# Differences of later sets made in the attentions and the second half's rings, and the mix's gating one product later

## The chip, the cores and the metric

The kernel runs on one core of one Trainium2 chip, all in float32. The metric is the device time of one execution in microseconds (us): 1691.08, the median of three runs (1689.67 to 1693.02).

## The reference

One layer of a decoder trunk: sequence 2048, width 1024, 16 query heads and 2 key/value heads of 64, window 128. A modulation of x by the condition c comes first, then one wide projection, an attention and a pooling branch side by side, a gated mix of the two, an output projection and a LayerNorm.

```python
shift, scale, gate = split(silu(c) @ w_ada + b_ada, 3)
u = x * (1 + scale) + shift
q, k, v, a_gate, p_in, p_gate, m_a, m_p = split(u @ w_in, offsets)
a = sliding_window_sink_attention(q, k, v, sinks, bias, mask) * silu(a_gate)
a = a @ w_attn_proj
p = grouped_linear(multiscale_causal_pool(p_in), w_pool_mix)
p = (p * pool_scale * silu(p_gate)) @ w_pool_proj
y = sigmoid(m_a) * a + sigmoid(m_p) * p
y = (y @ w_out) * (1 + gate)
x = layer_norm(alpha * x + y, ln_gain, ln_bias)
```

## The kernel before

**Products.** Every float32 operand is split into a high and a low part, and a product is three matmuls for each of four blocks of 128 rows, 12 of 128x512 in all (`product`, L317). The high part is a cast on ScalarE; the low part, source minus high part, is a subtraction on VectorE or GpSimd (`low`, L131; `pair_split`, L304; `half_split`, L310).

**Seven products for eight.** Matrices are multiplied two by two in blocks, with sums and differences of blocks, so that seven products do for eight. The activations are the "sets" B11, T1, T2, B21, T3, B22 and T4, each of which holds a high and a low part; T1 to T4 are differences of the blocks B11, B12, B21 and B22. The weights' differences are made on GpSimd (`sum1` L269, `mid` L273 and L274, `late` L278). The results stand in banks of PSUM, four called mm and two called lg. Some additions on VectorE stand between the products: `b = c + p5` after T2 (L368) and `p5 = c + p5` after T3 (L390). T3 and T4 add into the bank c that these additions read, so the next product into c waits for them.

**Sets from memory.** The inputs of later stages lie in device memory as blocks: `ain_d` (attention times its gate), `pin_d` (pool), `wo_d` (the output projection's weights), each in four slices. `sums_to` (L199) makes the differences of one slice: it loads four blocks of 256 KB into two tiles called spare, makes T1, T2, T4 and T3 as four subtractions of 128x512 on GpSimd, and stores each. `set_steps` (L509) loads and splits a finished set shortly before its stage.

**Stages.** The sequence is worked in two halves, s = 0 and 1:

1. Head, and the first half's rings: gates, keys, values and the first queries.
2. Attention of half 0 (`attention`, L774). It runs 67 steps n; one step is a block of scores, softmax, transposes and values for one pair of heads. Between these, 13 "fills" (products for pool, queries and merge gates) are spread evenly, 93 products in all. Each fill's weights are split up to three products ahead (`splits`).
3. The second half's rings (`second_phase`, L1465), five groups of 14 ticks; a tick is the end of one product. Beside the products, side work hangs on given ticks (`hooks`): here `sums_to` for all slices of `ain_d[0]` and `pin_d[0]`, and the scaling of `wo` by 1 + gate.
4. Attention of half 1.
5. The mix (from L1560): six phases. The first finishes the gates; then the attention's and the pool's projections for half 0 and for half 1 (two groups of 14 ticks each); then the output projection and the norm. Its side work before is `sums_to` for `ain_d[1]`, `pin_d[1]` and `wo_d`, one slice every 8 ticks from tick 2.

**Order.** The compiler's scheduler orders an engine's instructions by its own estimate. Operations called through `pe`, `act`, `dve`, `pool` and `sp` (class `Ordered`, L51) are pinned behind the instruction that was written before them for that engine; those called as `nc.vector` or `nc.scalar` are free. All loads and stores named here are issued by the queue of SP, in order. An engine works its instructions in order, and one that waits holds those behind it. `defer(k, f)` writes f k ticks later; `later(n, f)` in the attention writes f at step n.

**Gating in the mix.** In `attn_quad` (L611) a product's result is multiplied by its sigmoid gate into a tile `wide` (L618); in `pool_quad` (L622) it is multiplied by its gate (L627) and added to `wide` (L629), which is then stored. Both are called at the tick at which the product ends. The gates are loaded by `gates_ahead` (L599), which writes the sigmoid (L607) right after the load. In `back` (L341) two such quads make a group, in the order T2, B21 for each, then T3, B22 for each, then T4 for each.

Of the kernel before, what the change touches and what calls it, by code (L numbers as in the profile page):

```python
# [60 lines left out]
def kernel(  # L61
# [137 lines left out]
    def sums_to(ph, store, i, load, work=None, sums=True):  # L199

        b = []

        def x(r, c):
            return b[r][:, c * CH : (c + 1) * CH]

        def fetch():
            b.extend((ph.spare(), ph.spare()))
            b.reverse()
            for r in (1, 0):
                load(b[r], r)  # L210

        def sub(out, a, c):
            return lambda: pool.tensor_tensor(x(*out), x(*a), x(*c), ALU.subtract)

        todo = [(0, fetch)]
        if work:
            todo += [(3, lambda: work(b[0], 0)), (3.5, lambda: work(b[1], 1))]
        made = [("B11", (0, 0)), ("B21", (1, 0)), ("B22", (1, 1))] if work else []
        if work and not sums:
            made.insert(1, ("B12", (0, 1)))  # L220
        puts = [(5 + 0.6 * n, *x) for n, x in enumerate(made)]
        if sums:
            at = 7.5 if work else 4
            for out, a, c, name in (
                ((0, 1), (0, 1), (0, 0), "T1"),
                ((1, 1), (1, 1), (0, 1), "T2"),
                ((1, 0), (1, 0), (1, 1), "T4"),
                ((0, 0), (1, 1), (0, 0), "T3"),
            ):
                todo.append((at, sub(out, a, c)))  # L230
                puts.append((at + 2.5, name, out))
                at += 1.5
# [108 lines left out]
    def back(ph, grp, opened, nxt, own, tick):  # L341
# [5 lines left out]
        for q, (a, b, c, w, *copy) in zip(grp, opened):  # L347
# [19 lines left out]
            if len(copy) < 2:  # L367
                nc.vector.tensor_tensor(b, c, p5, ALU.add)  # L368
# [17 lines left out]
        def with_t3(x):  # L386
# [3 lines left out]
            nc.vector.tensor_tensor(p5, c, p5, ALU.add)  # L390
# [14 lines left out]
        for q, b, c, p5 in st:  # L405
            w = half_split(ph, q.a22)
            product(c, w, "T4")
            tick()
            q.consume(ph, 1, 0, c)

# [188 lines left out]
    def gates_ahead(name, s, m, raw):  # L599
        g = {}  # L600

        def ahead(ph, turn):
            for mi, t in (((0, 0), (1, 1)), ((0, 1), (1, 0)))[turn]:
                x = g[mi, t] = ph.c("g")
                sp.dma_start(x, gates_d[name][s, m + mi, t])
                if raw:
                    nc.scalar.activation(x, x, AF.Sigmoid)  # L607

        return g, ahead

    def attn_quad(s, m):  # L611
        g, ahead = gates_ahead("ma", s, m, True)

        def consume(ph, mi, t, src):
# [3 lines left out]
            nc.vector.tensor_tensor(ta[k][:, t * CH : (t + 1) * CH], src, g.pop((mi, t)), ALU.mult)  # L618

        return Quad((wap[m], wap[m + 1]), consume, ahead)  # L620

    def pool_quad(s, m):  # L622
        gates, ahead = gates_ahead("mp", s, m, True)

        def consume(ph, mi, t, src):
            g = gates.pop((mi, t))
            nc.vector.tensor_tensor(g, src, g, ALU.mult)  # L627
            dst = ta[m + mi][:, t * CH : (t + 1) * CH]
            nc.vector.tensor_tensor(dst, g, dst, ALU.add)  # L629
            defer(3, lambda: sp.dma_start(y_d[s, m + mi, t], dst))  # L630

        return Quad((wpp[m], wpp[m + 1]), consume, ahead)
# [141 lines left out]
    def attention(ph, s, fills, post, opened):  # L774
# [690 lines left out]
    def second_phase(ph, opened, post, plan1):  # L1465
# [37 lines left out]
        hooks.setdefault((3, 0), []).append(lambda: ph.turns.clear())  # L1503
# [57 lines left out]
    with Pools("mix", spare=4, p=2, c=8) as ph:  # L1561
# [92 lines left out]
```

## Time and profile before

| what | us |
|---|---|
| median of three runs | 1691.08 |
| the profiled execution | 1693.3 |
| its span, first to last instruction | 1691.5 |
| TensorE busy | 1648.7 |
| VectorE busy | 1193.7 |
| ScalarE busy | 1030.0 |
| GpSimd busy | 988.5 |

In the rows of the profile PE is TensorE's matmul, PEld its load of weights, DVE VectorE, ACT ScalarE, POOL GpSimd, SP the engine that issues DMAs (SPq its queue). A row of a timeline gives the start in us from the span's start, the length, engine, line, operation, the tile written and those read, shapes, and how many such instructions are merged; in brackets the idle time of the engine before it and what ended that. A row of the busy times by stage gives the stage, its length, the busy time of PE, PEld, DVE, ACT and POOL (with counts), the granted share of TensorE's clock, the share of the DMA engines and GB/s. Line 57 stands for everything called through `Ordered`. The first attention runs from about 254 to 600 us, the second half's rings to 824, the second attention to 1176, the mix to the end.

### The profile page before, as it was taken

The page shows a single profiled execution, that of the slowest core. Times are in us where ns is not written, and L with a number is a line of the kernel's source. Part 1 is how long each engine was busy: PE and PEld are TensorE (multiplying, and loading weights), DVE is VectorE, ACT ScalarE, POOL GpSimd, SP SyncE. Part 2 cuts the span into 40 slices and gives each one's busy share as a digit, 9 for nine tenths or more (in the row PEclk, how much of TensorE's full clock was granted, in tenths as well). Part 3 has the DMA queues.
Part 4 walks back from the last instruction along what each step waited for, and adds up shares of the span by engine and source line. Part 5 has one row for each costly group of instructions (what it writes and reads, how often), then busy time and mean ns, then how long its engine had stood idle before and what let it go on. Part 6 is the DMA issues. An engine that isn't in the chain of part 4 may idle for free.

```text
span 1691.5 us, 24675 instructions
## 1 busy us (share of the span) xinstructions
PE 1648.7 (97%) x8058; PEld 1384.4 (82%) x8058; DVE 1193.7 (71%) x2132; ACT 1030.0 (61%) x2150; POOL 988.5 (58%) x734
## 2 busy tenths in 40 slices
PE   7999999999999999999999999999999999999997
PEld 6788888888888888888788888888878777887886
DVE  6856545676857657357567677676669897989877
ACT  4755457878778755335578777876646445644452
POOL 3343437586857828762476867496567576533442
PEclk9999999999999999999999999999999999999999
DMA  9688843343432478766533344234979797888443
GB/s 359 219 279 307 197 161 102 101 132 108 149 107 99 135 248 308 267 231 211 190 114 99 114 130 156 81 114 135 336 247 363 262 360 259 318 283 271 150 150 112
DMA packets 188849, 336.79 MB, mean 199 GB/s; under 512 B 18336, under 2 KB 44080, under 8 KB 188720
## 3 DMA queue, kind: packets, MB, share of 16 engines
q1 hardware_dynamic: 185600, 330.96, 57.3%
q10 hardware_dynamic: 3088, 4.23, 1.0%
q8 instruction: 64, 1.05, 0.2%
q14 instruction: 65, 0.53, 0.1%
q0 software_dynamic: 32, 0.02, 0.0%
HBM read 227.96 MB, written 110.33 MB: 200 GB/s over the span
## 4 chain that ended last, share of the span: by engine, by line
PE 74%; DVE 8%; DMA 7%; ACT 4%; issue 3%; POOL 3%; SPq 1%; POOLq 0%; DVEq 0%; ACTq 0%
PE mm L57 48%; PE lg L57 19%; PE pv L57 4%; PE pt L57 4%; DVE w_set L132 1%; DMA ain_T<-spare 1%; ACT L L57 1%; DMA g<-ma_d 1%; DMA g<-mp_d 1%; DVE w_set L57 1%; DVE set_T L57 1%; POOL W L269 1%; DMA spare<-pin_B 1%; DVE L L57 1%; ACT w_set L57 1%
## 5 line engine op out<-in xcount | busy, mean ns | idle before, releaser
L57 PE MATMUL mm<-set_B,w_set 128*128 128x512 f32 x2664 | 655.8, 393 | 2.2 <-DVE w_set L132 1.2
L57 PEld LDWEIGHTS mm<-set_B,w_set 128*128 128x128 f32 x2664 | 497.1, 189 | 107.0 <-DVE w_set L132 2.4
L57 PE MATMUL mm<-set_T,w_set 128*128 128x512 f32 x1824 | 455.5, 396 | 5.9 <-DVE mm L57 3.9
L57 PE MATMUL lg<-set_T,w_set 128*128 128x512 f32 x1704 | 412.6, 392 | 10.5 <-DVE p L390 4.4
L57 PEld LDWEIGHTS mm<-set_T,w_set 128*128 128x128 f32 x1824 | 336.7, 189 | 76.2 <-DVE mm L57 6.5
L57 PEld LDWEIGHTS lg<-set_T,w_set 128*128 128x128 f32 x1704 | 319.9, 189 | 81.8 <-ACT w_set L306 5.2
L132 DVE TENSOR_TENSOR w_set<-W,w_set 128x1024 fp32r<-128x1024 f32 x137 | 197.8, 1445 | 142.3 <-ACT w_set L306 129.3
L306 ACT CAST w_set<-W 128x1024 fp32r<-128x1024 f32 x137 | 143.8, 1050 | 212.7 <-PE mm L57 124.3
L57 POOL TENSOR_TENSOR w_set<-W,w_set 128x512 fp32r<-128x512 f32 x120 | 157.3, 1318 | 116.9 <-ACT w_set L57 112.0
L269 POOL TENSOR_TENSOR W<-W,A 128x512 f32<-128x512 f32 x46 | 74.1, 1610 | 232.5 <-DMA A<-in_win_dram 63.5
L57 DVE TENSOR_TENSOR o<-pv,o 64x128 f32<-64x128 f32 x256 | 72.1, 282 | 133.7 <-ACT o L57 127.3
L57 POOL TENSOR_TENSOR spare<-spare 128x512 f32<-128x512 f32 x68 | 124.0, 1826 | 31.5 <-DMA spare<-pin_B 12.2
L57 POOL TENSOR_TENSOR W<-W 128x512 f32<-128x512 f32 x82 | 108.3, 1336 | 53.2 <-DVE sm L57 31.0
L57 ACT ACTIVATE L<-L,nm 128x257 f32<-128x257 f32 (+1 forms) x256 | 127.2, 499 | 9.3 <-DVE nm L57 3.7
L278 POOL TENSOR_TENSOR W<-W 128x512 f32<-128x512 f32 x46 | 72.8, 1583 | 95.9 <-DVE w_set L132 83.5
L57 DVE CUSTOM_DVE_ANT_0 L<-lg,bt,nsink 128x256 f32<-128x256 f32 (+1 forms) x256 | 111.7, 473 | 21.3 <-PE lg L57 11.9
L57 ACT CAST w_set<-W 128x512 fp32r<-128x512 f32 (+1 forms) x165 | 101.4, 628 | 20.9 <-POOL W L57 14.9
L273 POOL TENSOR_TENSOR W<-W 128x512 f32<-128x512 f32 x44 | 72.7, 1656 | 66.3 <-DVE w_set L132 57.2
L57 ACT COPY o<-pv 64x256 f32<-64x256 f32 x128 | 47.4, 370 | 75.9 <-PE pv L57 74.7
L57 DVE TENSOR_TENSOR ptl<-pt,pth 128x512 fp32r<-128x512 f32 (+1 forms) x128 | 85.7, 669 | 1.3 <-ACT pth L57 1.0
L274 POOL TENSOR_TENSOR W<-W 128x512 f32<-128x512 f32 x44 | 71.6, 1628 | 21.9 <-DMA W<-in_win_dram 18.9
L57 ACT ACTIVATE L<-L,sm 128x256 f32<-128x256 f32 (+1 forms) x128 | 64.3, 502 | 31.7 <-DVE sm L57 31.4
(230 smaller groups left out, 2398.2 us busy)
## 6 DMA issues: line engine op xcount, KB each, us to landing
W<-in_win_dram SPq DMA_DIRECT2D x42, 512.0 KB, 5.4
W<-in_win_dram SPq DMA_DIRECT2D x42, 256.0 KB, 3.7
A<-in_win_dram SPq DMA_DIRECT2D x42, 256.0 KB, 4.9
ag_d<-sig SPq DMA_DIRECT2D x32, 256.0 KB, 5.7
pg_d<-sig SPq DMA_DIRECT2D x32, 256.0 KB, 4.4
pg<-pg_d SPq DMA_DIRECT2D x32, 256.0 KB, 3.2
pin_B<-fin SPq DMA_DIRECT2D x32, 256.0 KB, 2.0
ag<-ag_d SPq DMA_DIRECT2D x32, 256.0 KB, 2.9
```

Of the source, the lines that this page charges most:

```text
L57: return lambda *args, **kw: self.tc.keep_in_program_order(op(*args, **kw))
L132: engine.tensor_tensor(dst, src, as32(hi), ALU.subtract)
L269: e.tensor_tensor(self.w[:, 1, :], self.w[:, 2, :], self.a22, ALU.add)
L273: e.tensor_tensor(x[:, 1, :], x[:, 1, :], x[:, 0, :], ALU.subtract)
L274: e.tensor_tensor(x[:, 2, :], x[:, 0, :], x[:, 2, :], ALU.subtract)
L278: e.tensor_tensor(x[:, 3, :], x[:, 3, :], x[:, 1, :], ALU.subtract)
L306: a.copy(by_two(hi), raw)
```

## The change

Four things change:

- **Where differences are made.** In each attention, `sums_to` now runs for three of the four slices of that half's `ain_d`, from steps 39, 56 and 61, at half a step for a tick. Its two tiles are the places of two query tiles (qs00, qs01). The second half's rings make the fourth slice of `ain_d[0]`, all of `pin_d[0]`, and now the differences of `wo` too, with other start ticks. The mix keeps only the fourth slice of `ain_d[1]` and the four of `pin_d[1]`, one every 14 ticks from tick 11. The tiles borrowed in the rings are given back a group earlier.
- **Start of an attention.** The first two splits are written ahead of the copy `seed(0)` and the load of the Exp table, the third behind the copy p5.
- **Gating in the mix.** A product's gating is written when the next product is consumed (`one_behind`), the last one at the first tick after the group. Gatings, and the additions L368 and L390 in these groups, are pinned.
- **Small steps.** The sigmoid is written a tick later than the load of its gate; y is stored two ticks after the gating rather than three.

```diff
-    def sums_to(ph, store, i, load, work=None, sums=True):
+    def sums_to(ph, store, i, load, work=None):
...
-            todo += [(3, lambda: work(b[0], 0)), (3.5, lambda: work(b[1], 1))]
+            todo += [(4, lambda: work(b[0], 0)), (4.5, lambda: work(b[1], 1))]
...
     def back(ph, grp, opened, nxt, own, tick):
...
-                nc.vector.tensor_tensor(b, c, p5, ALU.add)
+                (dve if q.ahead else nc.vector).tensor_tensor(b, c, p5, ALU.add)
...
-            nc.vector.tensor_tensor(p5, c, p5, ALU.add)
+            (dve if q.ahead else nc.vector).tensor_tensor(p5, c, p5, ALU.add)
...
             q.consume(ph, 1, 0, c)
+        defer(1, use_up)
...
-                    nc.scalar.activation(x, x, AF.Sigmoid)
+                    defer(1, lambda x=x: nc.scalar.activation(x, x, AF.Sigmoid))
...
+    unused = []
+
+    def use_up():
+        while unused:
+            unused.pop()()
+
+    def one_behind(use):
+
+        def consume(ph, mi, t, src):
+            use_up()
+            unused.append(lambda: use(ph, mi, t, src))
+
+        return consume
...
-            nc.vector.tensor_tensor(ta[k][:, t * CH : (t + 1) * CH], src, g.pop((mi, t)), ALU.mult)
+            dve.tensor_tensor(ta[k][:, t * CH : (t + 1) * CH], src, g.pop((mi, t)), ALU.mult)
-        return Quad((wap[m], wap[m + 1]), consume, ahead)
+        return Quad((wap[m], wap[m + 1]), one_behind(consume), ahead)
...
-            nc.vector.tensor_tensor(g, src, g, ALU.mult)
+            dve.tensor_tensor(g, src, g, ALU.mult)
             dst = ta[m + mi][:, t * CH : (t + 1) * CH]
-            nc.vector.tensor_tensor(dst, g, dst, ALU.add)
-            defer(3, lambda: sp.dma_start(y_d[s, m + mi, t], dst))
+            dve.tensor_tensor(dst, g, dst, ALU.add)
+            defer(2, lambda: sp.dma_start(y_d[s, m + mi, t], dst))
-        return Quad((wpp[m], wpp[m + 1]), consume, ahead)
+        return Quad((wpp[m], wpp[m + 1]), one_behind(consume), ahead)
...
         bts = {0: bias_tile(0)}
+        for i in (-3, -2):
+            for j in splits.get(i, ()):
+                split(j)
+        seed(0)
         act.activation(warm, mhalf, AF.Exp)
-        seed(0)
         p5 = st[0][3] = tp.tile([P, CH], F32, tag="p5", bufs=2, name="p5")
         act.copy(p5, st[0][1])
-        for i in range(-3, 0):
-            for j in splits.get(i, ()):
-                split(j)
+        for j in splits.get(-1, ()):
+            split(j)
+
+        def sums_between(n0, i):
+            for offset, f in [(0, rooms), *sums_to(ph, ain_d[s], i, load_raw(ain_d[s], i))]:
+                later(n0 + int(offset / 2), f)
+
+        def rooms():
+            ph.turns["spare"] = iter([kvp.tile([P, D], F32, tag=f"qs0{t}", name=f"room{t}") for t in range(2)])
+
+        for i, n0 in enumerate((39, 56, 61)):
+            sums_between(n0, i)
...
-        for raw in (ain_d[0], pin_d[0]):
-            for i in range(4):
-                side.append(sums_to(ph, raw, i, load_raw(raw, i)))
+        for raw, i in ((ain_d[0], 3), *((pin_d[0], i) for i in range(4))):
+            side.append(sums_to(ph, raw, i, load_raw(raw, i)))
...
-                False,
...
-        for start, todo in zip((14, 18.5, 23, 27.5, 32, 36.5, 41, 45.5, 57, 61, 65, 69), side):
+        for start, todo in zip((14, 18, 22, 26, 30, 34, 39, 44, 50), side):
...
-        hooks.setdefault((3, 0), []).append(lambda: ph.turns.clear())
+        hooks.setdefault((2, 0), []).append(lambda: ph.turns.clear())
...
-        for n, (raw, i) in enumerate((raw, i) for raw in (ain_d[1], pin_d[1], wo_d) for i in range(4)):
+        for n, (raw, i) in enumerate([(ain_d[1], 3), *((pin_d[1], i) for i in range(4))]):
             for offset, f in sums_to(ph, raw, i, load_raw(raw, i)):
-                at = int(2 + 8 * n + offset)
+                at = int(11 + 14 * n + offset)
```

More of the change, by code (lines that the diff above doesn't have):

```diff
@@ L216, in sums_to @@
         if work:
-            todo += [(3, lambda: work(b[0], 0)), (3.5, lambda: work(b[1], 1))]
+            todo += [(4, lambda: work(b[0], 0)), (4.5, lambda: work(b[1], 1))]
         made = [("B11", (0, 0)), ("B21", (1, 0)), ("B22", (1, 1))] if work else []
-        if work and not sums:
-            made.insert(1, ("B12", (0, 1)))
         puts = [(5 + 0.6 * n, *x) for n, x in enumerate(made)]
[L222 to L232, printed above, removed]
+        at = 7.5 if work else 4
+        for out, a, c, name in (
+            ((0, 1), (0, 1), (0, 0), "T1"),
+            ((1, 1), (1, 1), (0, 1), "T2"),
+            ((1, 0), (1, 0), (1, 1), "T4"),
+            ((0, 0), (1, 1), (0, 0), "T3"),
+        ):
+            todo.append((at, sub(out, a, c)))
+            puts.append((at + 2.5, name, out))
+            at += 1.5
         for at, name, z in puts:
```

## The prediction

> **What bounds the kernel now.** I read the page first, then the list of TensorE's waits, then the busy time by stage, then the timeline around each place where TensorE stood. The page:
>
> ```profile
> span 1691.5 us, 24675 instructions
> PE 1648.7 (97%) x8058; PEld 1384.4 (82%) x8058; DVE 1193.7 (71%) x2132; ACT 1030.0 (61%) x2150; POOL 988.5 (58%) x734
> ```
>
> TensorE is the bound. The change takes no product away, so all it can give or cost is time in which TensorE stands, or runs at less than the full clock. The waits of PE alone (us in total, times, longest), and then the stages in which PE is not full (length; PE busy; DVE, ACT, POOL; granted clock; DMA):
>
> ```profile
> PE lg L57 <- DVE p L390: 4.4, 3, 2.2
> PE lg L57 <- DVE w_set L132: 4.0, 1, 4.0
> PE mm L57 <- DVE mm L57: 3.9, 4, 1.6
> ```
>
> ```profile
> 254.00:265.00 11.00, 9.58 (x39) 7.44 (x38) 1.46 (x7) 6.39 (x15) 7.38 (x6) 0.84 0.27 75
> 265.00:560.00 295.00, 291.95 (x1591) 251.49 (x1590) 207.53 (x589) 228.73 (x637) 211.74 (x175) 1.00 0.36 115
> 560.00:600.00 40.00, 39.18 (x211) 33.26 (x211) 25.80 (x69) 26.95 (x70) 31.21 (x25) 1.00 0.43 141
> 600.00:824.00 224.00, 224.00 (x995) 185.34 (x994) 136.00 (x131) 103.75 (x148) 119.23 (x78) 1.00 0.75 256
> 824.00:835.00 11.00, 9.71 (x44) 7.45 (x43) 2.86 (x8) 7.24 (x14) 6.07 (x6) 1.00 0.49 162
> 835.00:1135.00 300.00, 297.72 (x1632) 256.89 (x1631) 213.15 (x591) 234.42 (x643) 213.82 (x170) 1.00 0.36 115
> 1135.00:1176.00 41.00, 40.56 (x220) 34.77 (x220) 27.07 (x69) 27.07 (x70) 31.27 (x25) 1.00 0.41 135
> 1215.00:1250.00 35.00, 30.77 (x124) 24.50 (x123) 28.26 (x24) 18.93 (x25) 22.24 (x13) 0.90 0.85 302
> 1320.00:1335.00 15.00, 12.76 (x50) 10.12 (x49) 14.86 (x16) 2.10 (x2) 11.57 (x8) 0.89 0.85 287
> 1370.00:1416.00 46.00, 43.48 (x187) 34.38 (x187) 42.42 (x36) 21.39 (x29) 30.18 (x17) 1.00 0.79 281
> 1520.00:1530.00 10.00, 8.52 (x38) 6.78 (x37) 9.93 (x12) 3.15 (x3) 2.91 (x2) 1.00 1.05 361
> ```
>
> What a stage loses is its length less PE's busy time, plus the share of the clock that was not granted. In the mix that gives 4.23 + 0.10 x 35 = 7.7 us, 2.24 + 0.11 x 15 = 3.9, 2.5 and 1.5: together 15.6. The start of the first attention (254 to 265) loses 1.42 + 0.16 x 11 = 3.2, that of the second (824 to 835) 1.3. The rest of the attentions loses 3.05 + 0.82 + 2.28 + 0.44 = 6.6, and the second half's rings (600 to 824) nothing. So the change has about 20 us to win, and most of it lies in the mix.
>
> The clock's part can be doubted. The Trainium skill (TensorE: Matmul & The Clock Gate, Part 1) has the clock halved only after an idle window of about 3.4 us; by it a stall of 2.24 us, the one in 1320 to 1335, would cost no clock, and the sum below would be 1.7 us smaller. The row with 0.89 says that this one did, and I go by the row.
>
> **What the mix waits for.** Timeline of the largest stall (start, us, engine):
>
> ```profile
> 1209.01 1.23 DVE L132 TENSOR_TENSOR w_set<-W,w_set 128x1024 fp32r<-128x1024 f32 x1 [2.27 <-ACT w_set L306]
> ...
> 1227.50 4.52 POOL L57 TENSOR_TENSOR spare<-spare 128x512 f32<-128x512 f32 x2
> ...
> 1228.56 2.31 DVE L132 TENSOR_TENSOR w_set<-W,w_set 128x1024 fp32r<-128x1024 f32 x1
> ...
> 1235.90 1.27 DVE L618 TENSOR_TENSOR wide<-mm,g 128x512 f32<-128x512 f32 x2
> ...
> 1237.10 0.67 DVE L390 TENSOR_TENSOR p<-lg,p 128x512 f32<-128x512 f32 x1
> 1237.81 0.69 DVE L618 TENSOR_TENSOR wide<-p,g 128x512 f32<-128x512 f32 x1
> ...
> 1238.41 2.28 DVE L132 TENSOR_TENSOR w_set<-W,w_set 128x1024 fp32r<-128x1024 f32 x1
> ...
> 1240.75 2.07 PE L57 MATMUL lg<-set_T,w_set 128*128 128x512 f32 x4 [4.00 <-DVE w_set L132]
> ```
>
> Two things make VectorE late here. Three gatings (1.27 + 0.69 us) and an addition stand in its queue before the low part (1238.41) for which TensorE waits. And that low part takes 2.28 us, as does the one at 1228.56 beside a GpSimd difference, where the one at 1209.01 took 1.23. So a difference that meets such an instruction costs VectorE about 1.05 us. The second stall is the order alone:
>
> ```profile
> 1325.81 1.75 DVE L629 TENSOR_TENSOR wide<-g,wide 128x512 f32<-128x512 f32 x1
> ...
> 1327.48 0.68 DVE L390 TENSOR_TENSOR p<-lg,p 128x512 f32<-128x512 f32 x1
> ...
> 1328.30 4.48 PE L57 MATMUL lg<-set_T,w_set 128*128 128x512 f32 x12 [2.24 <-DVE p L390]
> ```
>
> The addition p, which frees the bank lg for T4, stands behind a gating of 1.75 us.
>
> **The change, part by part.**
>
> Gating one product later. No instruction is added. The gating of a product is written behind the addition of the next, and that order is now binding. The stall at 1328 goes (3.9 us; I count 3.6), and so does 1520 to 1530, which has the same picture (1.5; I count 1.2). At 1240 the low part comes earlier only by the gatings that move behind it, 1.3 to 2.0 us of 4.0; a stall left at 2 us keeps half its clock loss. I take 4.5 of 7.7, with 0 and 7.7 as ends. A bank is held until the next product is consumed, two to three products; the same bank is asked for again a whole group later, so no product waits for that. The sigmoid, one tick later on ScalarE, adds no instruction; a g that came late would now hold VectorE, since the order binds. I put 1 us against it (0 to 4, the longest wait above).
>
> Differences out of the mix: 12 sets become 5, 28 of 48 GpSimd differences go, with 56 DMAs of 256 KB. Those at ticks 15 to 19 of the mix stay (the fourth set of the attention's output, second half), so the first stall keeps its four. Later they come every 14 ticks and not every 8, and after tick 82 not at all. Between 1370 and 1416 VectorE is busy for 42.42 of 46 us, which is where 1.05 us a meeting counts; of the 2.5 us lost there I take 1.5 as won, between 0 and 2.5. Sum of the mix: 4.5 + 3.6 + 1.5 + 1.2 - 1 = 9.8.
>
> Start of the attentions. Copies and casts on ScalarE before:
>
> ```profile
> 253.69 0.57 ACT L57 COPY mm<-mm 128x512 f32<-128x512 f32 x1 [2.00 <-PE mm L57]
> 256.36 0.59 ACT L57 COPY p<-mm 128x512 f32<-128x512 f32 x1 [2.10 <-PE mm L57]
> 256.84 1.66 ACT L57 CAST w_set<-W 128x512 fp32r<-128x512 f32 x3
> ...
> 257.51 0.73 PE L57 MATMUL mm<-set_T,w_set 128*128 128x512 f32 x2 [0.80 <-ACT w_set L57]
> ...
> 258.87 3.97 PE L57 MATMUL mm<-set_T,w_set 128*128 128x512 f32 x10 [0.62 <-POOL w_set L57]
> ```
>
> ScalarE stands 2.00 and 2.10 us for TensorE with two splits behind it that wait for nothing. Written first, they fit into those 4 us, their GpSimd low parts too. I take 2.7 of 3.2 in the first attention and 0.5 of 1.3 in the second, where the keys must also be loaded first, which the change leaves alone. Together 3.2 (0 to 4.5).
>
> Differences into the attentions: 12 on GpSimd in each, 12 loads and 12 stores with them. A low part on GpSimd is the nearest in shape there:
>
> ```profile
> L57 POOL TENSOR_TENSOR w_set<-W,w_set 128x512 fp32r<-128x512 f32 x50 | 65.9, 1324 | 48.8 <-ACT w_set L57 46.9 <-PE mm L57 1.9
> ```
>
> So 12 x 1.32 = 16 us an attention. One step is about 5.2 us (254 to 600 over 67 steps). The first set (steps 41 to 43) falls in the stage in which GpSimd is busy for 211.74 of 295 us, the third (63 to 65) behind 580, where 31.21 of 40 leave it 8.8 us. The second (58 to 60, from about 560 on) falls where ScalarE already waits for GpSimd:
>
> ```profile
> 566.78 3.00 POOL L57 TENSOR_TENSOR W<-W 128x512 f32<-128x512 f32 x2
> 568.12 0.63 ACT L57 CAST w_set<-W 128x512 fp32r<-128x512 f32 x1 [4.24 <-POOL W L57]
> ...
> 573.52 1.29 POOL L57 TENSOR_TENSOR w_set<-W,w_set 128x512 fp32r<-128x512 f32 x1
> ...
> 576.14 2.60 POOL L57 TENSOR_TENSOR w_set<-W,w_set 128x512 fp32r<-128x512 f32 x2
> ...
> 578.38 2.89 PE L57 MATMUL mm<-set_B,w_set 128*128 128x512 f32 x12
> ...
> 581.11 0.84 PE L57 MATMUL mm<-set_T,w_set 128*128 128x512 f32 x3
> ```
>
> The low parts of three products follow each other: the first ends at 574.81 and is wanted at 578.38, the second ends at 577.4 and is wanted at 581.11, the third ends at 578.74 and is wanted a product (2.9 us) later, at 584.0. Their cover is 3.6, 3.7 and 5.3 us. By the code's order the two differences of step 58 (2.6 us) come ahead of the first and the second, that of step 59 ahead of the third (together 4.0), that of step 60 behind it. So the cover holds, by about 1 us. Queued behind the differences are sum1, mid and late, for whose results ScalarE's casts wait, and with them the softmax.
>
> The queue of SP gets waits too. At step 39 the loads wait for the last scores of two q tiles; at step 61 the loads of the third set wait for a store of the second that has just been issued into the same tiles. Weight loads and the gate's store stand behind, and ScalarE's next copy into the one tile raw waits for that store. What such a transfer takes:
>
> ```profile
> DMA to landing us min/median/max: 2.0/5.4/8.8
> ```
>
> Against a step of 5.2 us that is 0 to 3.6 us. The ends for an attention are 0 and 5.3 + 3.6 = 8.9. I take 1 each, nearer to 0, because the cover holds by these rows: 2.
>
> Second half's rings: 32 differences become 36, in 50 ticks and not 57; 12 loads fewer, 12 stores more for wo and 12 fewer for the attention's output. PE is full (224.00), so nothing can be won. GpSimd is busy 119 of 224 us. I put 0.5, between 0 and 5.3 (four more differences, uncovered).
>
> **Sum:** 9.8 + 3.2 - 2 - 0.5 = 10.5 us. The profiled execution took 1693.3 us, 1.8 more than its span, and would take 1682.8. It lies 2.2 above the median of the runs, 1691.08; from that median the same sum gives 1680.6, and I predict **1680.5**.
>
> **Rivals.**
>
> *GpSimd's backlog in the attentions (slower).* If the second set's four differences find no cover, ScalarE's cast waits 4.24 + 5.3 us, and the softmax behind it stops TensorE for 5.3 us in each attention, with 3.5 us of clock as in 1215 to 1250: 2 x 8.8 = 17.6 us against 9.8 + 3.2 - 0.5 = 12.5 won, so 1696. It decides as soon as the lag that the differences add passes the cover of 3.6 us. For it: the 4.24 above, and a margin of only 1 us. Against: a stall of TensorE gives GpSimd time to catch up, and from 580 on it has idle time. Chance 0.13, 0.11 of it slower by over 0.2%.
>
> *The order is not what it says.* The low parts keep their freedom in VectorE's order. If they stay behind the additions, the first stall stays, and 1370 with it: 3.6 + 1.2 + 3.2 - 3.5 = 4.5 won, 1686.6. For it: four differences stay at that stall. Against: 1.96 us of gatings leave the place in front of it. Chance 0.14, a quarter of it within 0.2%.
>
> *VectorE is blocked in the attentions instead.* 24 differences at 1.05 us are 25 us of VectorE's time there; with half of that on the path the 12.5 us are gone: 1691. Against it: a low part on GpSimd takes 1.32 us there, in the mix a difference up to 2.3 (4.52 for two), so the two engines meet little in an attention. Chance 0.05. The rule that speaks for it is in the Trainium skill (SBUF — State Buffer, Who interferes with whom): a VectorE instruction with two inputs in SBUF and a GpSimd one that reads SBUF share one read interface, and the later one blocks. The mix's 1.23 and 2.31 agree with it.
>
> *All stalls of the mix and of the starts go, at no cost:* 15.6 + 4.5 = 20.1, so 1671. Chance 0.08.
>
> **How the numbers follow.** My forecast (1675 to 1686) has 0.60. A measurement can tell 0.2%, 3.4 us. Faster: 0.60 + 0.08 + 0.10 = 0.78; within 0.2%: 0.04 + 0.05 + 0.02 = 0.11; slower: 0.11. The range goes from 1671 to 1693. It leaves out half of the last case (0.04) and nearly all of the backlog (0.13), and takes in the other ends.
>
> **What would show it.** Right: no wait of PE for the addition p in the mix; 28 differences fewer there; the first casts of an attention before its copies; low parts at steps 58 to 62 still ahead of their products. Wrong: a wait of PE for pth or for GpSimd's low parts near 570 and 1145, or a wait of VectorE for g.

## The result and the profile after

The changed kernel took 1696.34 us (median; 1692.8 to 1700.94), the kernel before 1691.35 beside it: a ratio of 1.0027, 95% interval 1.0017 to 1.0037. It is slower by 0.27%, 15.8 us above the forecast and outside its range. The page of the profiled execution:

```profile
span 1695.4 us, 24670 instructions
PE 1647.3 (97%) x8058; PEld 1384.8 (82%) x8058; DVE 1179.4 (70%) x2132; ACT 1025.3 (60%) x2146; POOL 974.2 (57%) x734
```

TensorE (PE) is still the bound, with the same 8058 entries. VectorE and GpSimd have each lost 14 us of work, and it bought nothing. What PE waits for in the changed kernel (us in total, times, longest):

```profile
PE lg L57 <- DVE w_set L132: 13.2, 10, 2.6
...
PE mm L57 <- DVE mm L57: 6.2, 5, 2.1
...
PE mm L57 <- DVE sm L57: 2.1, 1, 2.1
```

(Lines are now the changed kernel's: L605 is the sigmoid, L303 is the cast of `pair_split`, L310 that of `half_split`, L387 the addition p.) The waits for the addition p, 4.4 us before, are gone, as the forecast had it. In their place stand ten waits for a low part (w_set, L132) in bank lg: 13.2 us, against one of 4.0. Nine of them, 12.6 us, lie in the mix. The other two rows hold a new wait of 2.1 us at the end of each attention. By stage, the changed kernel (length; PE, PEld, DVE, ACT and POOL busy; granted clock; DMA):

```profile
254.00:265.00 11.00, 11.00 (x54) 9.25 (x53) 3.05 (x13) 8.22 (x23) 7.39 (x6) 1.00 0.38 121
...
560.00:600.00 40.00, 37.16 (x189) 31.11 (x188) 22.55 (x59) 25.17 (x66) 35.18 (x29) 0.96 0.58 194
...
1135.00:1176.00 41.00, 38.52 (x203) 32.90 (x202) 25.20 (x65) 25.83 (x68) 36.21 (x30) 0.96 0.58 198
...
1250.00:1300.00 50.00, 47.15 (x206) 38.34 (x206) 35.00 (x33) 25.67 (x33) 21.14 (x14) 1.00 0.75 262
1300.00:1350.00 50.00, 50.00 (x222) 41.42 (x221) 39.12 (x38) 24.63 (x34) 29.88 (x18) 1.00 0.75 264
1350.00:1400.00 50.00, 45.71 (x201) 37.17 (x200) 45.38 (x45) 28.68 (x39) 25.68 (x14) 1.00 0.87 310
```

The last three stages in the kernel before:

```profile
1250.00:1300.00 50.00, 50.00 (x222) 41.44 (x221) 38.41 (x32) 28.18 (x36) 36.18 (x22) 1.00 0.93 329
1300.00:1350.00 50.00, 47.76 (x204) 39.09 (x204) 44.09 (x39) 22.06 (x30) 33.99 (x19) 0.97 0.75 261
1350.00:1400.00 50.00, 48.32 (x211) 39.06 (x210) 49.04 (x43) 27.33 (x37) 32.08 (x16) 1.00 1.00 366
```

The starts gained what was forecast: 254 to 265 loses nothing now (3.2 before), 824 to 835 loses 0.43 (1.3). The ends of the attentions lost: 2.84 + 0.04 x 40 = 4.4 us (0.82 before) and 2.48 + 0.04 x 41 = 4.1 (0.44), so 7.3 in all, where 2 were put down. In the mix 1300 to 1350 has become full, as forecast, but 1250 to 1300, which was full, loses 2.85, and 1350 to 1400 loses 4.29 and not 1.68.

For all kernels below there is one more measure, **late starts**: the interval from the start of one matmul to the next, less its usual length (0.227 us for 512 columns), summed over a stage of the one profiled execution of each kernel. It holds idle time and lost clock together. Late starts at the attentions' ends count from 290 us after an attention's first scores.

### The profile page after: what moved, and what is told of

It reads as the page before. It is cut to its first block, busy times and chain, and to the rows that moved or that the text cites. A ratio compares the mean times of both kernels' runs of the same rounds, so it can differ in the third digit from the quotient of the medians.

```text
span 1695.4 us, 24670 instructions
## 1 busy us (share of the span) xinstructions
PE 1647.3 (97%) x8058; PEld 1384.8 (82%) x8058; DVE 1179.4 (70%) x2132; ACT 1025.3 (60%) x2146; POOL 974.2 (57%) x734
## 3 DMA queue, kind: packets, MB, share of 16 engines
q8 instruction: 64, 1.05, 0.3%
## 4 chain that ended last, share of the span: by engine, by line
PE 76%; DVE 8%; DMA 5%; ACT 4%; issue 3%; POOL 2%; SPq 1%; POOLq 0%; DVEq 0%; ACTq 0%
PE mm L57 49%; PE lg L57 20%; PE pv L57 4%; PE pt L57 3%; DVE w_set L132 1%; DVE wide L57 1%; DMA head_T<-in_wada_dram 1%; DVE set_T L57 1%; ACT L L57 1%; SPq L57 1%; DMA g<-mp_d 1%; DMA g<-ma_d 1%; DVE w_set L57 1%; ACT g L605 1%; DVE L L57 1%
## 5 line engine op out<-in xcount | busy, mean ns | idle before, releaser
L57 PE MATMUL lg<-set_T,w_set 128*128 128x512 f32 x1704 | 412.9, 392 | 14.7 <-DVE w_set L132 13.2
L132 DVE TENSOR_TENSOR w_set<-W,w_set 128x1024 fp32r<-128x1024 f32 x137 | 192.0, 1403 | 148.7 <-ACT w_set L303 139.8
L303 ACT CAST w_set<-W 128x1024 fp32r<-128x1024 f32 x137 | 143.9, 1050 | 201.7 <-PE mm L57 154.9
L57 POOL TENSOR_TENSOR spare<-spare 128x512 f32<-128x512 f32 x48 | 77.7, 1626 | 10.9 <-ACT spare L57 5.5
```

What stands on the lines that cost most here:

```text
L57: return lambda *args, **kw: self.tc.keep_in_program_order(op(*args, **kw))
L132: engine.tensor_tensor(dst, src, as32(hi), ALU.subtract)
L303: a.copy(by_two(hi), raw)
```

## Where the ends of the attentions lose

Timeline of the changed kernel (start, us, engine, line, operation):

```profile
567.90 1.28 POOL L57 TENSOR_TENSOR room<-room 128x512 f32<-128x512 f32 x1
569.26 1.29 POOL L57 TENSOR_TENSOR room<-room,room 128x512 f32<-128x512 f32 x1
...
574.43 1.29 POOL L57 TENSOR_TENSOR W<-W 128x512 f32<-128x512 f32 x1
...
575.76 0.62 ACT L57 CAST w_set<-W 128x512 fp32r<-128x512 f32 x1 [2.17 <-POOL W L57]
576.40 0.37 ACT L57 COPY o<-pv 64x256 f32<-64x256 f32 x1
...
576.81 0.58 DVE L57 TENSOR_TENSOR o<-pv,o 64x128 f32<-64x128 f32 x2 [3.49 <-ACT o L57]
...
579.52 0.68 DVE L57 TENSOR_TENSOR mm<-mm,p 128x512 f32<-128x512 f32 x1
...
580.26 0.96 PE L57 MATMUL mm<-set_T,w_set 128*128 128x512 f32 x3 [2.08 <-DVE mm L57]
```

Read it downwards. The two new differences (room, 2.6 us) stand on GpSimd, with three other instructions, ahead of the weights' difference W. ScalarE's cast of W waits 2.17 us for it, and holds the copy o; VectorE stands 3.49 us for o; so its addition mm comes at 579.52, and PE waits 2.08 us. The low parts, whose cover the prediction had worked out, are in time.

## Where the mix loses

The same kernel at the stall in 1250 to 1300:

```profile
1273.43 0.63 ACT L605 ACTIVATE g<-g 128x512 f32<-128x512 f32 x1
...
1273.97 1.04 ACT L57 CAST set_B<-set_B 128x1024 fp32r<-128x1024 f32 x1
1274.90 1.05 ACT L303 CAST w_set<-W 128x1024 fp32r<-128x1024 f32 x1
...
1275.04 1.22 DVE L57 TENSOR_TENSOR set_B<-set_B 128x1024 fp32r<-128x1024 f32 x1 [2.66 <-ACT set_B L57]
...
1276.18 0.68 DVE L57 TENSOR_TENSOR wide<-mm,g 128x512 f32<-128x512 f32 x1
1276.78 0.68 DVE L57 TENSOR_TENSOR p<-lg,p 128x512 f32<-128x512 f32 x1
...
1277.38 0.68 DVE L57 TENSOR_TENSOR wide<-mm,g 128x512 f32<-128x512 f32 x1
...
1277.97 1.41 DVE L57 TENSOR_TENSOR set_T<-set_T 128x1024 fp32r<-128x1024 f32 x1
...
1279.31 1.75 DVE L57 TENSOR_TENSOR wide<-p,g 128x512 f32<-128x512 f32 x1
1280.99 1.21 DVE L132 TENSOR_TENSOR w_set<-W,w_set 128x1024 fp32r<-128x1024 f32 x1
...
1282.25 1.20 PE L57 MATMUL lg<-set_T,w_set 128*128 128x512 f32 x4 [2.58 <-DVE w_set L132]
```

The cast that the low part needs ended at 1275.95. The low part began 5 us later, behind an addition, three gatings and the low part of a set (set_T); and VectorE had stood 2.66 us for ScalarE's cast of another set (set_B) just before these. The same place in the change without its gating part (e1_no_gating):

```profile
1270.70 1.04 ACT L303 CAST w_set<-W 128x1024 fp32r<-128x1024 f32 x1
...
1271.77 1.23 DVE L132 TENSOR_TENSOR w_set<-W,w_set 128x1024 fp32r<-128x1024 f32 x1 [0.94 <-ACT w_set L303]
...
1272.91 0.68 DVE L387 TENSOR_TENSOR p<-lg,p 128x512 f32<-128x512 f32 x1
```

There the low part follows its cast at once and the addition comes behind it. So two things differ: when ScalarE's casts come, and where the low parts stand in VectorE's order. The experiments were to tell which edit makes them so.

## The experiments

All ratios are to the kernel before, run beside it on the same chip. "Low parts behind" counts, in the order of VectorE that the scheduler built, the low parts of fourth operands (L310) that stand behind the second addition of their group, out of 16 in the eight gated groups.

| kernel | median us | ratio (95%) | late starts in the mix, us | at the attentions' ends | low parts behind |
|---|---|---|---|---|---|
| before | 1691.35 | 1 | 18.4 | 1.9, 1.3 | 0 |
| changed | 1696.34 | 1.0027 (1.0017 to 1.0037) | 17.7 | 5.9, 5.2 | 8 |
| e1_no_gating | 1681.72 | 0.9951 (0.9937 to 0.9966) | 4.0 | 5.8, 3.6 | 1 |
| e2_gating_only | 1717.17 | 1.0159 (1.0140 to 1.0178) | 42.0 | 1.9, 1.2 | 9 |
| e3_start_only | 1687.43 | 0.9980 (0.9969 to 0.9991) | 20.5 | 1.9, 1.2 | 0 |
| e4_no_second_set | 1694.87 | 1.0026 (1.0016 to 1.0036) | 26.4 | 1.9, 1.2 | 8 |
| e5_late_free | 1691.38 | 1.0004 (0.9991 to 1.0016) | 15.8 | 5.9, 5.1 | 8 |
| e6_pinned_at_once | 1695.11 | 1.0031 (1.0019 to 1.0043) | 16.9 | 5.8, 3.6 | 8 |
| e7_low_first | 1693.76 | 1.0023 (1.0012 to 1.0035) | 15.4 | 4.3, 5.2 | 4 |
| e8_no_gating_no_second | 1685.19 | 0.9963 (0.9950 to 0.9977) | 15.7 | 1.9, 1.2 | 2 |
| e9_two_ticks_later | 1682.17 | 0.9945 (0.9933 to 0.9957) | 9.2 | 2.4, 1.6 | 1 |
| e10_sigmoid_at_once | 1686.00 | 0.9977 (0.9965 to 0.9989) | 8.1 | 5.8, 3.6 | 2 |
| e11_sigmoid_alone | 1690.75 | 0.9997 (0.9988 to 1.0006) | 15.1 | 4.2, 3.6 | 8 |
| e13_one_tick_later | 1680.16 | 0.9930 (0.9911 to 0.9949) | 9.6 | 2.2, 1.2 | 1 |
| e14_gating_sigmoid_at_once | 1696.69 | 1.0040 (1.0025 to 1.0055) | 24.0 | 1.8, 1.3 | 1 |
| e15_gating_and_starts | 1693.63 | 1.0019 (1.0007 to 1.0031) | 19.6 | 1.9, 1.2 | 1 |
| e16_low_parts_pinned | 1705.43 | 1.0081 (1.0067 to 1.0094) | 29.9 | 5.8, 3.6 | 0 |
| e17_pinned_and_later | 1706.98 | 1.0090 (1.0077 to 1.0104) | 36.1 | 2.2, 1.2 | 0 |

The last column does not set the loss by itself: the kernel before has 0 and late starts of 18.4 us, e1_no_gating has 1 and 4.0 us.

A difference of two ratios below is given in us of 1691; its own uncertainty is about 0.0017, 3 us.

### The parts alone

**e1_no_gating**: the changed kernel with the gating part taken back.

```diff
-                (dve if q.ahead else nc.vector).tensor_tensor(b, c, p5, ALU.add)
+                nc.vector.tensor_tensor(b, c, p5, ALU.add)
...
-                    defer(1, lambda x=x: nc.scalar.activation(x, x, AF.Sigmoid))
+                    nc.scalar.activation(x, x, AF.Sigmoid)
...
-        return Quad((wap[m], wap[m + 1]), one_behind(consume), ahead)
+        return Quad((wap[m], wap[m + 1]), consume, ahead)
```

> The changed kernel with its gating part undone (gating at once, additions and gatings free in VectorE's order, sigmoid and store as before); moved differences and the start of the attentions stay. Theory A (the pinned, later gating is the wait that took the mix's old place): the mix loses 10 us less than in the changed kernel, about 1687, and PE's waits for w_set L132 in the mix fall from 13.2 us to under 6. Rival B (the new ticks of the differences make the mix's stalls, the order is harmless): 1696 or above, with the same stalls.

Measured 0.9951, further down than theory A had it, and PE's waits for low parts on VectorE in the mix are gone. The moved differences and the starts are a gain, and the gating part makes a loss of it: 1.0027 - 0.9951 is 12.9 us.

**e2_gating_only**: the kernel before with the lines above the other way round, and nothing else.

> The kernel before with the gating part alone. Theory A: slower by 3 to 8 us, 1694 to 1699, PE waiting for w_set L132 near the T3 and T4 products of each group. Rival B: faster by 5 to 6 us, 1685 to 1686, as the prediction had it for the order.

Measured 1.0159, 26.9 us slower, far outside what was expected of any theory. With the mix's 48 differences still there the gating part costs twice as much.

**e3_start_only**: the kernel before with the splits ahead of the copies.

```diff
+        for i in (-3, -2):
+            for j in splits.get(i, ()):
+                split(j)
+        seed(0)
         act.activation(warm, mhalf, AF.Exp)
-        seed(0)
```

> The kernel before with the start of the attentions alone. Theory A (the start gives what the trace shows): faster by 4.5 us, about 1686.5. Rival (what is won at the start is waited for later in the same attention): within 1.5 us of 1691.

Measured 0.9980, 3.4 us faster, where the prediction had 3.2.

### The second set in the attentions

**e4_no_second_set**: the changed kernel with the second set of each attention made in the rings and the mix.

```diff
-        for i, n0 in enumerate((39, 56, 61)):
+        for i, n0 in ((0, 39), (2, 61)):
```

> The changed kernel, but each attention makes the first and the third set only; the second is made in the second half's rings and in the mix (start ticks closer). Theory A (the second set's differences hold GpSimd's late, and with it ScalarE and VectorE, near 577 and 1155): those two stalls go, 7 us faster than the changed kernel, about 1689, less what denser side work costs elsewhere (0 to 3). Rival (the stalls come from the third set's loads in SP's queue): they stay, 1696.

**e8_no_gating_no_second**: the same edit in e1_no_gating.

> The changed kernel without its gating part (1681.7) and with each attention making only the first and the third set. Theory A: the stalls near 577 and 1155 go, 7 us; the mix, whose VectorE is not held by the order, bears the added set at a cost of 0 to 3: 1675 to 1678. Rival (the added sets cost as much where they go): 1681 or above.

The late starts at the attentions' ends went back to those of before (1.9 and 1.2) in both, so the second set makes them. The time did not follow: 1.0026 and 0.9963. The mix gives it back, 26.4 against 17.7 us of late starts, and 15.7 against 4.0. So theory A was right on the stalls and wrong on the time, and e8 came out as its rival had it (1681 or above): by the time, a set costs where it goes about what it costs the attention.

**e9_two_ticks_later** and **e13_one_tick_later**: e1_no_gating with the second and third set later.

```diff
-        for i, n0 in enumerate((39, 56, 61)):
+        for i, n0 in enumerate((39, 58, 63)):
```

> The change without its gating part (as in e1_no_gating), and the differences of the second and third set made two steps later in each attention (from steps 58 and 63 on, not 56 and 61). Theory G (the two differences on GpSimd stand ahead of the attention's own product there, ScalarE's cast waits for it, and VectorE's addition comes late, at 577 and 1156 us): the sum of late matmul starts at an attention's end falls from 5.8 and 3.6 us towards 2 and 1.2, the time to 1675 to 1679. Rival (the set costs its work on VectorE and GpSimd wherever it stands): it stays at 1680 to 1683.

In e13_one_tick_later the starts are 39, 57 and 62.

> The change without its gating part (as in e1_no_gating), and the second and third set made one step later in each attention (from steps 57 and 62 on). Two steps later (e9_two_ticks_later) the late starts at the attentions' ends fell from 5.8 and 3.6 us to 2.4 and 1.6, but those after them rose from 1.6 to 3.5 us and in the mix from 4.0 to 9.2 us, so 1682.2 against 1681.7. Theory G with a place between: the differences on GpSimd are clear of the attention's last product, and VectorE's order in the rings behind is that of e1_no_gating; 1675 to 1679. Rival (where one gains the other gives back): 1680 to 1683.

Timeline of e9_two_ticks_later at the same product:

```profile
570.68 1.29 POOL L57 TENSOR_TENSOR W<-W 128x512 f32<-128x512 f32 x1
...
573.18 0.62 ACT L57 CAST w_set<-W 128x512 fp32r<-128x512 f32 x1
...
575.14 1.29 POOL L57 TENSOR_TENSOR room<-room 128x512 f32<-128x512 f32 x1
...
576.52 0.69 DVE L57 TENSOR_TENSOR mm<-mm,p 128x512 f32<-128x512 f32 x1
...
577.39 0.86 PE L57 MATMUL mm<-set_T,w_set 128*128 128x512 f32 x3
```

W is made ahead of the difference, the cast waits for nothing, the addition is early, and PE does not wait. So the chain of the attentions' ends is shown. The time was 0.9945 and 0.9930: not told apart from 0.9951, since late starts behind the attentions came in exchange (3.5 and 2.4 us in the second half's rings against 1.6, 9.2 and 9.6 in the mix against 4.0). The rival was nearer. What makes these was not pursued.

### The gating part taken apart

**e5_late_free**: the changed kernel; gatings late, but gatings and additions no longer pinned.

```diff
...
-            dve.tensor_tensor(ta[k][:, t * CH : (t + 1) * CH], src, g.pop((mi, t)), ALU.mult)
+            nc.vector.tensor_tensor(ta[k][:, t * CH : (t + 1) * CH], src, g.pop((mi, t)), ALU.mult)
```

> The changed kernel with the gating still one product later, but its gatings and the two additions free in VectorE's order. In the order that the scheduler then writes, the low part for the second quad's T3 stands right behind the addition p, not four places behind it. Theory A (it is the place of that low part, behind a pinned addition and the late gatings, that stops PE): the mix loses 4 to 7 us, about 1682 to 1685. Rival C (a later gating alone costs, since banks and gates are held longer): as the changed kernel, 1694 to 1697.

**e6_pinned_at_once**: pinned, but written when the product ends.

```diff
...
-        return Quad((wap[m], wap[m + 1]), one_behind(consume), ahead)
+        return Quad((wap[m], wap[m + 1]), consume, ahead)
```

> The changed kernel with gatings and additions pinned, but the gating at once and not one product later. The low part for the second quad's T3 stands right behind the addition p here too. Theory A: 1682 to 1687. Rival D (pinning alone costs, whatever stands where): 1694 to 1697.

**e7_low_first**: the changed kernel with the second quad's third operand split ahead of the addition.

```diff
...
+        cut(0)
         for x in range(len(st)):
             third(x)
             with_t3(x)
+            if x + 1 < len(st):
+                cut(x + 1)
```

> The changed kernel, gating late and pinned, with one thing moved: the split of the third block of the second quad is written before the first quad's B22, so that its low part stands ahead of the addition p in VectorE's order. Theory A: the stalls at the second quad's T3 go (1279, 1440 and the like), those at T4 (1364, 1524) may stay: about 1688, between 1684 and 1691. Rivals C and D: no change, 1694 to 1697.

Measured: 1.0004, 1.0031 and 1.0023, with 15 to 17 us of late starts in the mix. Theory A missed in all three. e6 came out as rival D had it (pinning alone costs), e7 stayed nearly where it was, and e5 lies between its two. The late starts say that something all of them keep makes most of the loss in the mix. They keep the sigmoid a tick later.

**e10_sigmoid_at_once**: the changed kernel with that one line put back. **e11_sigmoid_alone**: e1_no_gating with that one line alone.

```diff
-                    defer(1, lambda x=x: nc.scalar.activation(x, x, AF.Sigmoid))
+                    nc.scalar.activation(x, x, AF.Sigmoid)
```

> The changed kernel, pinned late gating and all, with one line put back: the sigmoid is issued with the load of g, not one tick later. Theory E (it is the sigmoid's place on ScalarE that pushes the fourth operands' low parts behind the additions in VectorE's order): the sum of late starts in the mix falls from 17.7 us to some 5 to 8, the time to 1682 to 1686. Theory A (the pinned, late gating does it): 1693 to 1697, as the changed kernel.

> The change without its gating part (as in e1_no_gating, 1681.7), with that part's one line on the sigmoid alone: issued one tick later. Theory E: the low parts stand behind the additions, the sum of late starts in the mix rises from 4.0 us to 12 to 18, the time is 1690 to 1696. Theory A: as without it, 1680 to 1683.

This line makes the larger part of the gating's loss. With the differences moved, the sigmoid's tick costs 0.9997 - 0.9951, 7.8 us, without the rest of the gating, and 1.0027 - 0.9977, 8.5 us, with it. The times lie at the edges of what theory E expected, the late starts (8.1 and 15.1 us) about where it had them; theory A is out by 7 to 8 us in both. The rest of the gating part costs 4.4 us (0.9977 - 0.9951) to 5.1 (1.0027 - 0.9997), and with the sigmoid late e5 and e6 split that: pinning alone costs 1.0031 - 0.9997, 5.7 us; lateness alone 1.0004 - 0.9997, 1.2 us, which is within the uncertainty. VectorE's waits for ScalarE between 1200 and 1560 us, in the changed kernel and then in e10_sigmoid_at_once:

```profile
DVE w_set L132 <- ACT w_set L303: 51.0, 22, 4.3
...
DVE set_B L57 <- ACT set_B L57: 7.6, 11, 2.7
```

```profile
DVE w_set L132 <- ACT w_set L303: 41.9, 19, 4.2
...
DVE set_B L57 <- ACT set_B L57: 2.5, 6, 1.2
```

So with the later sigmoid VectorE stands 14 us more for these casts of ScalarE (9.1 + 5.1; in the pair e1 and e11 the same two rows grow by 8.8), and more low parts are built in behind the additions.

The traces show which cast moved. ScalarE of e10_sigmoid_at_once at the place of the stall above, 2.96 us earlier in time:

```profile
1260.67 1.05 ACT L57 CAST set_B<-set_B 128x1024 fp32r<-128x1024 f32 x1 [0.42 <-DMA set_B<-pin_B]
...
1264.18 1.99 ACT L605 ACTIVATE g<-g 128x512 f32<-128x512 f32 x3
```

Two halves of set_B are cast in this group. Here the second is cast as soon as it has landed, ahead of the group's eight sigmoids; in the changed kernel it comes at 1273.97, behind all eight, although its load was issued at the same place. This holds in all 18 kernels, for the second group of each of the mix's four gated phases: both casts ahead of the sigmoids where the sigmoid is issued at once, one of them behind all eight where it is a tick later. The sigmoids themselves run within 0.5 us of the same place. VectorE's low part of set_B then comes late too, and what is pinned behind it with it. No run moves that cast alone, so its share of the 8 us is not measured.

**e14_gating_sigmoid_at_once** and **e15_gating_and_starts**: the kernel before with the gating part less the later sigmoid, and the same with the starts.

```diff
...
-        return Quad((wap[m], wap[m + 1]), consume, ahead)
+        return Quad((wap[m], wap[m + 1]), one_behind(consume), ahead)
```

> The kernel before with the gating part alone, as in e2_gating_only (1717.2, late starts in the mix 42 us), but with the sigmoid issued with the load of g as before. Theory E (the sigmoid's step sets the place of the low parts, with or without the moved differences): the late starts in the mix fall from 42 us to 6 to 12, the time to 1679 to 1686, below the kernel before. Rival (with four times as many differences in the mix it is the pinned gatings that hold the low parts): it stays above 1700.

> The same with the splits ahead of the copies at the attentions' starts (e3_start_only) as well, so the change without any moved difference and without the later sigmoid. If the parts add up: 3.9 us less than e14_gating_sigmoid_at_once, so 1675 to 1682, as fast as the change without its gating or faster, and the moving of the differences has bought nothing that this order does not. Rival: the parts shift the order once more and it is above 1684.

The sigmoid's tick costs 1.0159 - 1.0040, 20.1 us, without the moved differences: the same sign, larger. But 1.0040 is no gain: the expected 1679 to 1686 missed, its rival (above 1700) as well, and the sum for e15 with it. What is left, in e14_gating_sigmoid_at_once:

```profile
1371.76 3.43 DVE L57 TENSOR_TENSOR wide<-g,wide 128x512 f32<-128x512 f32 x2
...
1373.00 1.04 ACT L306 CAST w_set<-W 128x1024 fp32r<-128x1024 f32 x1 [5.80 <-POOL W L269]
...
1375.12 0.68 DVE L57 TENSOR_TENSOR g<-lg,g 128x512 f32<-128x512 f32 x1
1375.72 1.68 DVE L132 TENSOR_TENSOR w_set<-W,w_set 128x1024 fp32r<-128x1024 f32 x1
...
1377.45 2.08 PE L57 MATMUL mm<-set_B,w_set 128*128 128x512 f32 x4 [4.91 <-DVE w_set L132]
```

At the end of a pool group the pinned gatings, some slowed from 0.68 to 1.7 us beside GpSimd's work, stand ahead of the next group's first low part, and TensorE waits 4.91 us for it, from 1372.54 on. Not all of that is theirs: the low part's cast came only at 1373.00, after ScalarE had stood 5.80 us for GpSimd's sum W, and ended at 1374.04. With its own 1.2 us the low part could not have been ready before about 1375.3, so some 2.7 us are GpSimd's and some 2.2 us the gatings'. That the pinning keeps the gatings there is argued; no run frees them in this arrangement. In e15 the starts add up (-3.6 us), and 1.0019 against 0.9977 for e10 says that moving the differences is worth 7 us there.

### Is it the order alone?

**e16_low_parts_pinned**: the changed kernel, later sigmoid and all, with the third and fourth operands' low parts written ahead of the additions and pinned. **e17_pinned_and_later**: with the starts 39, 57 and 62 as well.

```diff
...
+            if gated and x == 0:
+                for y in range(len(st)):
+                    cut(y)
...
+            if gated and x + 1 == len(st):
+                lasts = [half_split(ph, q.a22, d) for q, *_ in st]
             with_t3(x)
```

> The changed kernel with nothing put back (later sigmoid, pinned late gating, moved differences), but the low parts of the third and fourth operands of a gated group are written ahead of the additions and pinned there, so they stand ahead in VectorE's order. Theory E' (the later sigmoid costs because of the order that follows from it on VectorE, not because ScalarE is late): the waits for low parts go, the late starts in the mix fall from 17.7 us to 4 to 9, the time to 1682 to 1687. Rival (the later sigmoid makes ScalarE's casts themselves late, or gates late): the pinned low parts wait for them and hold VectorE, 1692 to 1700.

> The same, with the second and third set one step later in the attentions (steps 57 and 62, as in e13_one_tick_later). If the parts add up, the attentions' ends give back some 6 us more: 1676 to 1681. Rival: the gain comes back behind them, as in e9_two_ticks_later, 1682 to 1687.

Theory E' fell: no low part stands behind an addition now, and the kernel is slower still, by 1.0081 - 1.0027, 9.1 us, beyond its rival's range too. In e17 the attentions' ends gave back what was expected (2.2 and 1.2 us for 5.8 and 3.6), but the mix lost more (36.1 us for 29.9), and the time is that of e16. Timeline of e16_low_parts_pinned, and a row of its waits between 1200 and 1560 us:

```profile
1391.72 2.67 ACT L617 ACTIVATE g<-g 128x512 f32<-128x512 f32 x4 [2.25 <-DMA g<-ma_d]
...
1395.24 2.18 ACT L617 ACTIVATE g<-g 128x512 f32<-128x512 f32 x4
...
1398.26 1.04 ACT L303 CAST w_set<-W 128x1024 fp32r<-128x1024 f32 x1
...
1400.13 2.35 DVE L57 TENSOR_TENSOR w_set<-W,w_set 128x1024 fp32r<-128x1024 f32 x2
1401.40 1.79 PE L57 MATMUL lg<-set_T,w_set 128*128 128x512 f32 x4 [4.91 <-DVE w_set L57]
```

```profile
DVE set_B L57 <- ACT set_B L57: 20.1, 13, 4.2
```

Here eight sigmoids, the first of which waits 2.25 us for its gate, stand on ScalarE with two casts of sets ahead of the cast. It comes at 1398.26 for a product that began at 1394.52, and a low part in the right place comes only after it. So the low parts' place behind the additions does not explain the loss by itself: without it the kernel is slower. But e16 pins more than it moves, so it does not price that place either. That the later sigmoid costs 8 to 20 us is shown, that it makes VectorE wait for ScalarE is measured, and that it puts a cast of set_B behind the sigmoids is seen in every pair. How the loss divides between casts that come late and low parts that are built in behind additions stays open.

## Why the prediction was wrong

The parts as measured by ratios (starts from e3, moved differences from e1 less e3, the gating's order from e10 less e1, the sigmoid from the changed kernel less e10) against the terms of the sum:

| term | forecast, us | measured, us |
|---|---|---|
| starts of the attentions | -3.2 | -3.4 |
| moved differences: mix, attentions and rings | +1.0 (-1.5, +2, +0.5) | -4.9 |
| gating later and pinned: 1240, 1328, 1520 | -9.3 | +4.4 |
| sigmoid a tick later | +1.0 | +8.5 |
| sum | -10.5 | +4.6 |

- **What bounds the kernel** was right, and so were the starts. Two steps failed, both in the gating: one by 13.7 us, the other by 7.5.
- **"That order is now binding. The stall at 1328 goes"** is the larger of them. That stall went, with every wait of PE for the addition, but 9.3 us were put down as won and 4.4 to 5.1 were lost. e14_gating_sigmoid_at_once shows it without the sigmoid and without the moved differences. There the waits for the addition, 4.4 us, are gone. The stall at 1240, of which 4.5 of 7.7 us were to be won, is still there: 4.5 us of waiting against 4.0, with three gatings and an addition ahead of the low part as before. And PE waits 8.9 us for low parts in bank mm, against 1.2, some 2.7 of it GpSimd's doing. The edit rearranges eight groups, and three places in them were priced. The rival "the order is not what it says" had the stall at 1240 staying, but at a gain of 4.5 us in all. Pinning is what lost (5.7 us, e6 less e11, with the sigmoid late in both); gating later by itself did nothing that these runs can tell.
- **"The sigmoid, one tick later on ScalarE, adds no instruction"** is the other, and the one that turned a gain into a loss: with it put back the kernel takes 0.9977. It was priced by a gate that comes late (1 us, 0 to 4), and no wait of VectorE for a sigmoid shows in the changed kernel's mix. Its cost was 7.8 to 8.5 us here and 20.1 without the moved differences, with a cast of set_B built in behind the sigmoids.
- **The stalls were not the gating's to win.** With the differences moved and the gating as before, the late starts in the mix are 4.0 us, against 20.5 in e3. The sum gave the moved differences 1.5 us of this. "A difference that meets such an instruction costs VectorE about 1.05 us" was counted only between 1370 and 1416. What the removed differences freed for the other stalls, VectorE's time, GpSimd's or the queue of SP, no run tells apart.
- **"So the cover holds, by about 1 us"** was true of the low parts and missed the shorter cover: the prediction named ScalarE's casts and the softmax behind the differences, and set no price on them. The two waits came to 7.3 us, not 2. The rival of GpSimd's backlog had the first links of this chain, at 17.6 us; that its 1696 is the time measured is chance, since the loss that made it lies in the mix.
- **The rings** lost 0.7 us by late starts (0.4 to 1.1), where 0.5 were put down.
- Of the signs named for it, "no wait of PE for the addition p", the 28 differences fewer and the first casts came true, and the signs of being wrong stayed at or below where they were (PE waits 0.8 us for pth, 1.0 before). The time was still wrong: no sign watched the low parts of the other groups.

The fastest version tried is the change without its gating part and with the second and third set a step later (e13): 1680.16 us, 0.9930 (0.9911 to 0.9949). Leaving the gating part out is what it takes; the step's place is not told apart from e1.

## What to carry to other kernels

An instruction moved by a step is to be priced by what the scheduler then puts behind it on its own engine, not by its own length: here a sigmoid that adds no work cost 8 to 20 us, and in every pair of kernels a cast that had stood ahead of the sigmoids, and for which VectorE waits, was built in behind them. Where a scheduler places the free instructions, an edit at three stalls rebuilds all groups like them; so read every one of these groups in the built order, and check that cover is worked out for each instruction behind the moved work, the shortest first. When the sum of a change is wrong, make the two-by-two of its parts early: three kernels that varied the gating left the cause standing, because all of them kept one line.

## What was not expected of the hardware

The granted clock fell after some short stalls and not after others of the same length. In the changed kernel, a stall of 2.58 us at 1279 and one of 2.08 at 578 us:

```profile
578.00:583.00 5.00, 2.92 (x16) 2.61 (x16) 3.09 (x9) 3.38 (x9) 5.00 (x5) 0.86 0.53 177
...
1279.00:1284.00 5.00, 2.42 (x11) 1.65 (x11) 4.84 (x5) 0.00 (x0) 1.51 (x1) 1.00 0.14 39
```

So the loss of clock that the prediction read from one stall cannot be counted for each. The Trainium skill (TensorE: Matmul & The Clock Gate, Part 1) has the clock halved after an idle window of about 3.4 us; the 1.00 behind 2.58 us and the four matmuls in 2.08 us behind 4.91 us agree with it, the 0.86 behind 2.08 us does not. That section also has the window run freely. If what a stall costs depends on where in the window it falls, this could reconcile the two, but no run here tries it.
